# Two transformer blocks on one core: late norm sums, value projections in rows of tokens, and another order of the mixer's jobs

## The chip, the core and the metric

The kernel runs on one core of a Trainium2 chip. The metric is the device time of one execution in microseconds (us). The core has TensorE (PE, matrix products), VectorE (DVE), ScalarE (ACT), GpSimd (POOL) and SyncE (SP, which here only issues DMAs). Each engine works through its own queue in order and waits on semaphores for the others; transfers from HBM run on 16 DMA engines.

## The reference

256 tokens of width 2048 go through two blocks in float32. The first has what the change touches; the second (a convolution and RWKV-7 mixer and a gated feed-forward part) stays as it is.

```python
h = rmsnorm(x, g_mix) * (1 + sc1) + sh1            # sc1, sh1 from silu(c) @ w_ada + b_ada
proj = h @ w_in
q_a, k_a, v_a, q_b, k_b, v_b, qi, ki, wi, g_a, g_b = jnp.split(proj, offsets, axis=-1)
y_a = stick_breaking_attention(q_a, k_a, v_a)       # 8 heads of 128
y_b = dsa_attention(rope(q_b), rope(k_b), v_b,      # 8 heads of 128, the 64 best keys
                    rope(qi), rope(ki), wi)         # by an index score of 16 heads of 64
merged = sigmoid(g_a) * (y_a @ w_a) + sigmoid(g_b) * (y_b @ w_b)
x = x + (1 + gt1) * (merged @ w_o)
```

A stick-breaking head needs `z = q k^T`, the softplus of z under a mask, running sums of it over the keys (products with a triangle), an exponential, and the product with v. A sparse head needs `q k^T` plus the mask of the 64 best keys, a softmax, and the product with v.

## The kernel before, in words

Activations lie with features on the 128 partitions and the 256 tokens on the free axis. Each weight matrix comes in blocks of 2048 x 128, loaded by one DMA of 1 MB (`raw`) and split into a high and a low part (`whi` on ScalarE, `wlo` on VectorE). A **job** is one such block: for each of 16 slices of the contraction three matmuls (high x high, high x low, low x high), 48 in all, into one PSUM bank; then its epilogue `epi` is called. Four slices make a **unit** (12 matmuls). `run` writes out the program: unit by unit it first splits weights some units ahead (`pump_hi`, `pump_lo`), then emits the matmuls, at a job's end its epilogue, and then calls `advance`, one **tick**.

Side work is written as Python generators in the list `fill`. `advance` takes the first three of the list and lets each do one step, if its time has come; `yield n` means "not before n ticks from now", a bare `yield` one tick. So the order of instructions on every engine is fixed when the program is written; a step's instructions stand on TensorE's queue between two units. A job's `pre` is called before its first matmul; `drain(gens)` in it calls `advance` until the named generators have ended, with no unit between those ticks. The background generator `bg` (other modulation vectors, on VectorE) makes a step in four ticks of seven.

The **prologue** (`start`) computes the modulation columns sc1 and sh1 from 33.5 MB of `w_ada` in four groups of eight steps (`kq`) of two 0.5 MB chunks `ch` each, held in eight buffers. A step is done either by TensorE (those in `PEQ`; `m<-cb,ch`) or by VectorE (`fa<-ch,csil,fa`; its sums are closed on TensorE, `m<-cm,fa`, after the last such step). `finish(g)` makes four of the 16 slices of h. The generator `side` runs beside it, two steps for each `kq`: the sums of squares of x for the norm (squares on ScalarE, additions on GpSimd, sums over features on TensorE, inverse root on VectorE, `rx`), then `rope_tables` (cosines and sines, in 33 steps). The first jobs of w_in are in the group `h1`, whose units are interleaved with the last three groups: they pull the prologue along by `need`.

Jobs then follow in the order key/weight job, eight index query jobs, eight stick-breaking heads (q, k, v job each), eight sparse heads (q, k, v), gates with `w_a` and `w_b`, `w_o`. `v_epi` copies the values, turns them with two TensorE transposes a tick later, and copies them again. `sb_gen(h)` and `dsa_gen(h)` are created when a head's v job ends and wait until its values are there.

Of the kernel before, what the change touches and what calls it, by code (L numbers as in the profile page):

```python
# [123 lines left out]


class Job:
    def __init__(self, chunks, mv, n, epi, pre=None, outs=None, group=None, need=None, gate=False):
        self.chunks = chunks
        self.mv = mv
        self.n = n  # L130
        self.epi = epi
        self.pre = pre
        self.nk = sum(c[1] for c in chunks)
        self.outs = outs or [(0, self.nk)]
        self.group = group
        self.need = need
        self.gate = gate


class Builder:  # L140
# [258 lines left out]
    def run(self, jobs):  # L399
# [121 lines left out]
        for i, (j, ci, o, k, n) in enumerate(order):  # L521
            if j.gate:
                if (i - gi) % 4 == 0:
                    gated(i)
                continue
            if j.group == "h1":
                j.need(k + n)
                pump_dma()
            if self.lazy:
                pump_hi(i + LEAD)  # L530
                pump_lo(i + LOMIN)
                for x in range(LOMIN + 1, LEAD):
# [12 lines left out]
            hi, lo = wt.pop(i)  # L545
            for q in range(n):
                kk = k + q
                oi = next(x for x, (a0, n0) in enumerate(j.outs) if a0 <= kk < a0 + n0)
                a0, n0 = j.outs[oi]
                out = ps[id(j)][oi][:, :j.n]  # L550
                mh, ml = j.mv(kk)
                self.mm(out, hi[:, q], mh, start=(kk == a0), stop=False)
                self.mm(out, hi[:, q], ml, start=False, stop=False)
                self.mm(out, lo[:, q], mh, start=False, stop=(kk == a0 + n0 - 1))
            if k + n == j.nk:
                j.epi(*ps.pop(id(j)))
            self.advance()
# [167 lines left out]
    def kw_epi(self, ps):  # L725
        ki = self.rope(ps, self.cosi, self.sini)
        self.kz = [self.a(), self.a()]
        self.nc.vector.memset(self.kz[1][:, :S], 0.0)
        self.ts(self.kz[0][:, :S], ki[:, :S], self.pcol("kmask"))
        self.act(self.kz[1][32:64, :S], ki[0:32, :S])  # L730
        self.act(self.kz[1][96:128, :S], ki[64:96, :S])
        w = self.a()
        self.act(w[32:48, :S], ps[32:48, :S])

        def g():
            yield
            p = self.mps()
            for t in range(2):
                self.nc.tensor.transpose(p[:, 16 * t:16 * t + 16], w[32:48, 128 * t:128 * t + 128], self.ident[32:48, 32:48])
            self.wi = self.cp.tile([128, 32], F32, name="wi")  # L740
            self.ts(self.wi, p[:, 0:32], 0.25)
            yield

        self.g_kw = self.later(g())
# [43 lines left out]
        self.busy = False  # L788
        yield

    def v_epi(self, store, h):
        def epi(ps):
            t = self.a()
            self.act(t[:, :S], ps[:, :S])

            def g():
                yield
                p = self.mps()
                for k in range(2):
                    self.nc.tensor.transpose(p[:, 128 * k:128 * k + 128], t[:, 128 * k:128 * k + 128], self.ident)  # L800
                o = self.a()
                self.act(o[:, :S], p[:, :S])
                store[h] = o
                yield
            self.later(g())
        return epi

    def sb_gen(self, h):
# [26 lines left out]
        self.mm(cp[:, 256:384], tri, sp[:, 256:384])  # L835
        self.sub(zs, zs, cp[:, :384])
        self.act(zs, zs, AF.Exp)
        yield 3
        self.pv(zs, v, self.ya, h)
        yield  # L840

# [7 lines left out]

    def dsa_gen(self, h):  # L850
        scale = 128.0 ** -0.5
        while h not in self.vb or self.g_idx in self.fill:
            yield
        q, k, v = self.qb.pop(h), self.kb.pop(h), self.vb.pop(h)
        lp = self.mps()
# [24 lines left out]
    def build_mixer(self):  # L880
# [13 lines left out]
        self.qi, self.qa, self.ka, self.va, self.qb, self.kb, self.vb = {}, {}, {}, {}, {}, {}, {}  # L894
        self.ya, self.yb = {}, {}

        wj(self.kw_epi, group="h1")
        for j in range(8):
            wj(self.qi_epi(j), group="h1" if j < 3 else None)

        def start_idx():
            self.drain([self.g_kw])
            self.g_idx = self.later(self.index_gen())
# [15 lines left out]
        def with_gen(epi, make, lst):  # L919
            def f(ps):  # L920
                epi(ps)
                lst.append(self.later(make()))
            return f

        for hh in range(NH):
            wj(cp_epi(self.qa, hh), pre=start_idx if hh == 0 else None)
            wj(cp_epi(self.ka, hh))
            wj(with_gen(self.v_epi(self.va, hh), lambda hh=hh: self.sb_gen(hh), sbg))
        for hh in range(NH):
            wj(rp_epi(self.qb, hh))  # L930
            wj(rp_epi(self.kb, hh))
            wj(with_gen(self.v_epi(self.vb, hh), lambda hh=hh: self.dsa_gen(hh), dsg))

        mg = {}
        self.mg = mg
# [838 lines left out]
    def start(self):  # L1774
# [37 lines left out]
        h = self.h  # L1812

        def xnorm():
            pa, pb = self.mps(), self.mps()
            for i in range(KT):
                q = self.a()
                self.act(q[:, :S], x[i][:, :S], AF.Square)
                if i % 4:
                    nc.gpsimd.tensor_add(t[:, :S], t[:, :S], q[:, :S])  # L1820
                else:
                    t = q
                if i % 4 == 4 - 1:
                    for p, o in ((pa, 0), (pb, 128)):
                        self.mm(p[:, 0:64], t[:, o:o + 128], self.ones[:, 0:64], start=i == 4 - 1, stop=i == KT - 1)
                    yield
            v, y, q = self.tiny(), self.tiny(), self.tiny()
            self.ts(v[:, 0:1], pa[:, 0:1], 1.0 / D, EPS)
            self.ts(v[:, 1:2], pb[:, 0:1], 1.0 / D, EPS)
            self.rsq(y[:, :2], v[:, :2], q[:, :2], 3)  # L1830
            rps = self.bcast(y)
            self.rx = self.a()
            self.act(self.rx[:, :S], rps[:, :S])
            yield

        accs, sums = {}, {}
        side = self.chain(xnorm(), self.rope_tables())

        def accumulate(g, kq):
            if kq == 0:  # L1840
# [14 lines left out]
            for mi, m in enumerate((1, 0)):  # L1855
                for j in range(4):
                    o = ps[:, 256 * mi + 64 * j:256 * mi + 64 * j + 64]
                    c = slice(128 * j, 128 * j + 128)
                    if kq in pe:
                        b = 128 * PEK.index(kq)  # L1860
                        for kk in range(2):
                            self.mm(o, chunks[g, kq, m][:, kk, c], cb[:, b + 64 * kk:b + 64 * kk + 64],
                                    start=kq == pe[0] and kk + mi + j == 0, stop=kq == 7 and kk + mi + j == 5)
                    if kq == dve[-1]:
                        self.mm(o, accs[g][m][:, c], self.ones[:, 0:64], start=False, stop=kq == 7 and mi + j == 4)
            for _ in range(SPE if kq in pe else 0):
                next(side, None)
            fetch()
# [19 lines left out]
        def steps():  # L1888
# [8 lines left out]
                yield  # L1897
            for _ in side:
                pass
            nc.sync.dma_start(self.cm[:, 256:NCM], self.ap["cmask"][:, 256:NCM])  # L1900
            self.x = None
            self.enter(1)
# [48 lines left out]


_W = {
    "w_in": (89, 128, KT, 128), "w_ada": (D, 6 * D), "w_a": (KT, 128, 8, 128), "w_b": (KT, 128, 8, 128),
    "w_o": (KT, 128, KT, 128), "w_up": (2 * FT, 128, KT, 128), "w_down": (NQ, KT, 128, FQ, 128),
    "w_in_2": (52, 128, KT, 128), "lora": (8, 128, 4, 128), "w_out_2": (KT, 128, KT, 128),
    "w_gu_2": (2 * FT, 128, KT, 128), "w_down_2": (NQ, KT, 128, FQ, 128),
# [24 lines left out]
def layout(inp):  # L1982
# [11 lines left out]
    wi = w[:, o[8]:o[9]]  # L1994
    kw = np.concatenate([ki[:, :32], wi, np.repeat(z, 16, 1), ki[:, 32:], np.repeat(z, 32, 1)], 1)
    qi = w[:, o[6]:o[7]].reshape(D, 8, 2, 2, 32).transpose(0, 1, 3, 2, 4).reshape(D, 1024)
    cols = [kw, qi]
    for h in range(NH):
        for s in range(3):
            cols.append(w[:, o[s] + 128 * h:o[s] + 128 * h + 128])  # L2000
    for h in range(NH):
        for s in range(3, 6):
            cols.append(w[:, o[s] + 128 * h:o[s] + 128 * h + 128])
    for s in (9, 10):
        for j in range(KT):
            cols.append(w[:, o[s] + 128 * j:o[s] + 128 * j + 128])
    out["w_in"] = _blocks(np.concatenate(cols, 1))
    out["w_ada"] = np.ascontiguousarray(g["w_ada"][0])
    out["w_a"] = _blocks(g["w_a"][0])
    out["w_b"] = _blocks(g["w_b"][0])  # L2010
# [82 lines left out]
```

## Time and profile before

| what | us |
|---|---|
| median of 3 runs | 3025.03 |
| the runs | 3024.79, 3025.03, 3029.89 |
| profiled execution, its own time | 3029.85 |
| span from first to last instruction | 3028.1 |

The rows further down come from that one profiled execution. A row of a timeline has the start, the time, engine, source line, operation, output<-inputs, shapes and count, and in brackets how long the engine was idle before it and what ended that. Nearly all matmuls have line 271, a helper; `m` are small PSUM tiles, `g` those of jobs. A float32 matmul stands as two instructions. A matmul's busy time overlaps the next one's, so the rate is read from starts or from the pieces of the chain.

### The profile page before, as it was taken

The page shows a single profiled execution, that of the slowest core. Times are in us where ns is not written, and L with a number is a line of the kernel's source. Part 1 is how long each engine was busy: PE and PEld are TensorE (multiplying, and loading weights), DVE is VectorE, ACT ScalarE, POOL GpSimd, SP SyncE. Part 2 cuts the span into 40 slices and gives each one's busy share as a digit, 9 for nine tenths or more (in the row PEclk, how much of TensorE's full clock was granted, in tenths as well). Part 3 has the DMA queues.
Part 4 walks back from the last instruction along what each step waited for, and adds up shares of the span by engine and source line. Part 5 has one row for each costly group of instructions (what it writes and reads, how often), then busy time and mean ns, then how long its engine had stood idle before and what let it go on. Part 6 is the DMA issues. An engine that isn't in the chain of part 4 may idle for free.

```text
span 3028.1 us, 66212 instructions
## 1 busy us (share of the span) xinstructions
PE 2975.4 (98%) x27088; PEld 2944.3 (97%) x27088; DVE 2185.2 (72%) x4516; ACT 1573.9 (52%) x3214; POOL 161.6 (5%) x295
## 2 busy tenths in 40 slices
PE   7999999999999999999999999999999999999997
PEld 7999999999999999999999999999999999999997
DVE  6787798677887667676677867777577556566565
ACT  1256544444556556565567545444565555454454
POOL 1000000000210000000002000001000000000002
PEclk9799999999999999999999999999999999999998
DMA  9867677787875554555545433233445454554543
GB/s 343 307 219 250 220 261 264 255 288 263 316 261 184 179 190 168 202 181 177 189 163 188 160 116 116 89 108 125 140 151 197 167 198 173 202 181 167 198 162 129
DMA packets 123473, 594.18 MB, mean 196 GB/s; under 512 B 12832, under 2 KB 19360, under 8 KB 81056
## 3 DMA queue, kind: packets, MB, share of 16 engines
q1 hardware_dynamic: 103200, 518.60, 48.9%
q0 software_dynamic: 19968, 71.35, 7.4%
q8 instruction: 212, 3.47, 0.4%
q14 instruction: 93, 0.76, 0.1%
HBM read 585.68 MB, written 4.21 MB: 195 GB/s over the span
## 4 chain that ended last, share of the span: by engine, by line
PE 95%; DVE 3%; DMA 2%; ACT 0%; issue 0%; SPq 0%; POOL 0%; DVEq 0%; ACTq 0%; POOLq 0%
PE g L271 85%; PE m L271 9%; DMA ch<-w_ada 1%; DVE wlo L242 0%; DMA a<-xT 0%; DVE a L262 0%; DVE a L242 0%; PE m L1414 0%; DVE o L242 0%; DMA cm<-cmask 0%; DVE fa L262 0%; DMA raw<-w_up 0%; ACT a L229 0%; DVE acc L262 0%; DVE p L242 0%
## 5 line engine op out<-in xcount | busy, mean ns | idle before, releaser
L271 PE MATMUL g<-a,whi 128*128 128x256 f32 (+2 forms) x11920 | 2187.2, 285 | 2.4 <-ACT a L229 1.9
L271 PEld LDWEIGHTS g<-a,whi 128*128 128x128 f32 x11920 | 1845.7, 189 | 14.1 <-ACT a L229 2.0
L271 PE MATMUL g<-a,wlo 128*128 128x256 f32 (+3 forms) x5960 | 1684.1, 283 | 1.5 <-DVE wlo L242 1.5
L229 ACT ACTIVATE whi<-raw 128x512 fp32r<-128x512 f32 (+1 forms) x1852 | 1093.4, 617 | 519.3 <-PE g L271 495.5
L242 DVE TENSOR_TENSOR wlo<-raw,whi 128x512 fp32r<-128x512 f32 (+1 forms) x1852 | 1212.9, 681 | 132.2 <-ACT whi L229 130.8
L271 PEld LDWEIGHTS g<-a,wlo 128*128 128x128 f32 x5960 | 1127.1, 189 | 2.9 <-DVE wlo L242 2.6
L271 PE MATMUL g<-h,whi 128*128 128x256 f32 x1408 | 248.9, 281 | 0.0
L271 PE MATMUL g<-ex,whi 128*128 128x258 f32 x1232 | 227.1, 284 | 0.0
L271 PEld LDWEIGHTS g<-h,whi 128*128 128x128 f32 x1408 | 214.9, 188 | 0.0
L271 PE MATMUL g<-h,wlo 128*128 128x256 f32 x704 | 197.8, 281 | 0.0
L271 PEld LDWEIGHTS g<-ex,whi 128*128 128x128 f32 x1232 | 191.3, 190 | 0.0
L262 DVE SCALAR_TENSOR_TENSOR acc<-ra,csil,acc 128x512 f32<-128x512 f32 x240 | 182.1, 759 | 3.9 <-DMA ra<-w_ada 3.9
L229 ACT ACTIVATE a<-a 128x256 f32<-128x256 f32 (+5 forms) x303 | 120.9, 410 | 106.4 <-DVE a L242 79.6
L271 PE MATMUL g<-ex,wlo 128*128 128x258 f32 x616 | 174.9, 284 | 0.3 <-DVE wlo L242 0.3
L262 DVE SCALAR_TENSOR_TENSOR a<-a,pc 128x255 f32<-128x255 f32 (+5 forms) x340 | 163.6, 482 | 5.5 <-ACT a L229 0.5
L229 ACT ACTIVATE a<-a,pc 128x256 f32<-128x256 f32 (+2 forms) x214 | 116.8, 547 | 58.6 <-DVE a L242 53.2
L242 DVE TENSOR_TENSOR a<-g,rb 128x258 f32<-128x258 f32 x80 | 34.1, 426 | 154.4 <-PE g L271 154.4
L635 POOL TENSOR_TENSOR a<-a 128x256 f32<-128x256 f32 x59 | 54.1, 927 | 1673.1 <-ACT a L229 1618.2
L229 ACT ACTIVATE a<-g 128x256 f32<-128x256 f32 (+3 forms) x121 | 46.2, 384 | 179.8 <-PE g L271 179.6
L271 PEld LDWEIGHTS g<-h,wlo 128*128 128x128 f32 x704 | 135.2, 192 | 0.0
L271 PE MATMUL m<-p 64*64 64x64 f32 x3328 | 133.6, 219 | 0.1
L262 DVE SCALAR_TENSOR_TENSOR a<-a 128x256 f32<-128x256 f32 (+3 forms) x275 | 116.6, 424 | 11.7 <-ACT a L229 7.7
(171 smaller groups left out, 1848.3 us busy)
## 6 DMA issues: line engine op xcount, KB each, us to landing
raw<-w_in SPq DMA_DIRECT2D x141, 1024.0 KB, 5.8
raw<-w_up SPq DMA_DIRECT2D x88, 1024.0 KB, 4.9
raw<-w_down SPq DMA_DIRECT2D x128, 704.0 KB, 4.1
raw<-w_gu SPq DMA_DIRECT2D x88, 1024.0 KB, 4.9
ra<-w_ada POOLq DMA_DIRECT2D x128, 512.0 KB, 5.4
ch<-w_ada SPq DMA_DIRECT2D x64, 512.0 KB, 7.5
raw<-w_o SPq DMA_DIRECT2D x16, 1024.0 KB, 7.2
raw<-w_out SPq DMA_DIRECT2D x32, 512.0 KB, 3.6
```

What stands on the lines that cost most here:

```text
L229: self.nc.scalar.activation(out, in_, f, **kw)
L242: self.nc.vector.tensor_tensor(out, a, b, op)
L262: self.nc.vector.scalar_tensor_tensor(out, a, s, b, op0, op1)
L271: self.nc.tensor.matmul(out, l, r, start=start, stop=stop)
L635: self.nc.gpsimd.tensor_tensor(q[:, :n], q[:, :n], acc[:, :n], ALU.add)
```

## The change

1. `xnorm` no longer sums over features as squares come in: it keeps four partial sums and issues the eight matmuls once seven steps of the prologue have been emitted.
2. `rope_tables` isn't part of `side` any more. It is put into `fill` when the prologue's last step has been emitted, and the key/weight job drains it first.
3. Values: four heads make one **wide** job. The stationary operand is h (128 tokens), the moving one a slice of 512 weight columns; two PSUM banks take 128 tokens each. Six matmuls a slice, a unit is one slice, 16 units a job. Its epilogue copies eight pieces of 128 x 128; the transposes are gone.
4. Order: q and k of heads 0 and 1 (these four jobs are now the group `h1`), values of heads 0 to 3, key/weight job, eight index query jobs, q and k of heads 2 and 3, values of 4 to 7, q and k of 4 to 7; then values of sparse heads 0 to 3, their q and k, values of 4 to 7, their q and k. The index generator starts with head 2's q job.
5. `sb_gen(h)` and `dsa_gen(h)` are created in the epilogue of the head's k job; `dsa_gen` waits for the key instead of the value.
6. Two waits in ticks: four instead of one before the weight transposes of the key/weight job, four instead of three before the last product of a stick-breaking head.

```diff
+            if j.wide:
+                kk, last = k // 4, k + n == j.nk
+                wh, wl = (t.rearrange("p q c -> p (q c)") for t in (hi, lo))
+                mh, ml = j.mv(kk)
+                for t in range(2):
+                    out, c = ps[id(j)][t], slice(128 * t, 128 * t + 128)
+                    self.mm(out, mh[:, c], wh, start=kk == 0, stop=False)
+                    self.mm(out, mh[:, c], wl, start=False, stop=False)
+                    self.mm(out, ml[:, c], wh, start=False, stop=last)
...
         def g():
-            yield
+            yield 4
             p = self.mps()
...
+    def v_epi(self, store, h0):
+        def epi(*ps):
+            for h in range(4):
+                o = store[h0 + h] = self.a()
+                for t in range(2):
+                    self.act(o[:, 128 * t:128 * t + 128], ps[t][:, 128 * h:128 * h + 128])
...
         self.act(zs, zs, AF.Exp)
-        yield 3
+        yield 4
         self.pv(zs, v, self.ya, h)
...
-        while h not in self.vb or self.g_idx in self.fill:
+        while h not in self.kb or self.g_idx in self.fill:
...
+        def vj(s, h0, pre=None):
+            w = ap["w_v"][2 * s + h0 // 4]
+            jobs.append(Job([(w[g], KT) for g in range(4)], mvh, S, self.v_epi(self.vb if s else self.va, h0), pre,
+                            outs=[(0, 2 * KT), (2 * KT, 2 * KT)], wide=True))
+
+        def sbq(hh, group=None, pre=None):
+            wj(cp_epi(self.qa, hh), pre=pre, group=group)
+            wj(with_gen(cp_epi(self.ka, hh), lambda hh=hh: self.sb_gen(hh), sbg), group=group)
+
+        sbq(0, "h1")
+        sbq(1, "h1")
+        vj(0, 0)
+        wj(self.kw_epi, pre=lambda: self.drain([self.g_rope]))
+        for j in range(8):
+            wj(self.qi_epi(j))
+        sbq(2, pre=start_idx)
+        sbq(3)
+        vj(0, 4)
+        for hh in range(4, NH):
+            sbq(hh)
         for hh in range(NH):
-            wj(cp_epi(self.qa, hh), pre=start_idx if hh == 0 else None)
-            wj(cp_epi(self.ka, hh))
-            wj(with_gen(self.v_epi(self.va, hh), lambda hh=hh: self.sb_gen(hh), sbg))
-        for hh in range(NH):
+            if hh % 4 == 0:
+                vj(1, hh)
             wj(rp_epi(self.qb, hh))
-            wj(rp_epi(self.kb, hh))
-            wj(with_gen(self.v_epi(self.vb, hh), lambda hh=hh: self.dsa_gen(hh), dsg))
+            wj(with_gen(rp_epi(self.kb, hh), lambda hh=hh: self.dsa_gen(hh), dsg))
...
         def xnorm():
-            pa, pb = self.mps(), self.mps()
+            sums = []
             for i in range(KT):
                 q = self.a()
                 self.act(q[:, :S], x[i][:, :S], AF.Square)
                 if i % 4:
+                    t = sums[-1]
                     nc.gpsimd.tensor_add(t[:, :S], t[:, :S], q[:, :S])
                 else:
-                    t = q
+                    sums.append(q)
                 if i % 4 == 4 - 1:
-                    for p, o in ((pa, 0), (pb, 128)):
-                        self.mm(p[:, 0:64], t[:, o:o + 128], self.ones[:, 0:64], start=i == 4 - 1, stop=i == KT - 1)
-                    yield
+                    yield
+            while len(seen) < 7:
+                yield
+            pa, pb = self.mps(), self.mps()
+            for i, t in enumerate(sums):
+                for p, o in ((pa, 0), (pb, 128)):
+                    self.mm(p[:, 0:64], t[:, o:o + 128], self.ones[:, 0:64], start=i == 0, stop=i == 4 - 1)
+            yield
             v, y, q = self.tiny(), self.tiny(), self.tiny()
...
-        side = self.chain(xnorm(), self.rope_tables())
+        seen = []
+        side = xnorm()
...
+            self.g_rope = self.later(self.rope_tables())
```

The weights of w_in are laid out anew to match (73 blocks and `w_v` of 4 x 4 blocks of 1 MB).

## Rows read from the trace of the kernel before

**Rows 1.** Page, part 1: busy time (share of the span) x instructions.

```profile
PE 2975.4 (98%) x27088; PEld 2944.3 (97%) x27088; DVE 2185.2 (72%) x4516; ACT 1573.9 (52%) x3214; POOL 161.6 (5%) x295
```

**Rows 2.** Timeline of TensorE in the prologue.

```profile
48.37 20.71 PE L271 MATMUL m<-cb,ch 128*128 128x64 f32 x96 [0.90 <-DMA ch<-w_ada]
...
74.96 7.74 PE L271 MATMUL m<-cb,ch 128*128 128x64 f32 x64
...
95.12 7.06 PE L271 MATMUL m<-cb,ch 128*128 128x64 f32 x32 [3.27 <-DMA ch<-w_ada]
...
102.51 0.41 PE L271 MATMUL g<-a,wlo 128*128 128x256 f32 x1
...
104.43 0.41 PE L271 MATMUL g<-a,wlo 128*128 128x256 f32 x1
104.64 13.75 PE L271 MATMUL m<-cb,ch 128*128 128x64 f32 x64
```

**Rows 3.** Windows: length, then busy time of each engine, granted clock, DMA share, GB/s.

```profile
14.00:76.00 62.00, 56.84 (x262) 56.12 (x262) 46.38 (x107) 11.05 (x24) 7.08 (x10) 1.00 0.99 357
76.00:89.60 13.60, 13.03 (x112) 12.58 (x111) 12.69 (x22) 3.73 (x8) 0.00 (x0) 1.00 1.05 387
89.60:120.30 30.70, 27.15 (x126) 27.00 (x127) 20.47 (x36) 2.44 (x5) 1.60 (x3) 0.50 0.92 334
138.00:172.00 34.00, 33.22 (x281) 33.20 (x282) 33.35 (x67) 15.91 (x27) 3.17 (x6) 1.00 0.67 233
350.00:504.00 154.00, 154.00 (x1301) 153.59 (x1300) 133.37 (x268) 74.80 (x163) 13.19 (x25) 1.00 0.72 243
2236.60:2246.90 10.30, 6.53 (x27) 6.08 (x27) 9.65 (x28) 5.23 (x13) 0.00 (x0) 0.50 0.00 1
```

**Rows 4.** All waits of TensorE, 138 to 771 us: total, times, longest.

```profile
PE m L739 <- ACT a L229: 2.0, 1, 2.0
PE m L271 <- ACT sc L229: 1.5, 1, 1.5
```

**Rows 5.** Chain that ended last, in a sparse head: start, time, what.

```profile
372.10 7.08 PE g L271 x60
379.18 0.22 PE m L800 x2
```

**Rows 6.** Timeline of VectorE in the prologue.

```profile
22.33 0.16 DVE L258 TENSOR_SCALAR ty<-m 128x1 f32<-128x1 f32 x1 [10.02 <-PE m L271]
...
38.78 1.54 DVE L262 SCALAR_TENSOR_TENSOR fa<-ch,csil,fa 128x512 f32<-128x512 f32 x2 [0.98 <-DMA ch<-w_ada]
```

**Rows 7.** The chain that ended last, in the second block's mixer.

```profile
1636.60 9.03 PE g L271 x72
```

**Rows 8.** Groups by line and shape, TensorE, 1637 to 1645 us: busy, mean ns.

```profile
L271 PE MATMUL g<-a,whi 128*128 128x272 f32 x23 | 4.5, 288 | 0.0
```

**Rows 9.** Timeline of ScalarE: the copy at a stick-breaking head's q job's end.

```profile
238.67 0.38 ACT L229 ACTIVATE a<-g 128x256 f32<-128x256 f32 x1 [1.41 <-PE g L271]
```

**Rows 10.** The chain that ended last, around the first stick-breaking head.

```profile
202.46 0.49 ACT sc L229
...
202.97 1.28 ACT L229
...
206.09 0.53 ACT sc L229
...
206.65 0.57 DVE sc L262
...
207.25 0.90 DVE sc L242 x4
```

**Rows 11.** Timeline of TensorE at the second feed-forward part's start.

```profile
2241.72 0.58 PE L271 MATMUL g<-a,whi 128*128 128x258 f32 x1 [1.95 <-ACT a L229]
```

**Rows 12.** Timeline of VectorE: a sparse head's rotation.

```profile
371.47 1.29 DVE L242 TENSOR_TENSOR a<-g,a 64x256 f32<-64x256 f32 x3 [1.08 <-PE g L271]
372.80 0.42 DVE L242 TENSOR_TENSOR a<-a 128x256 f32<-128x256 f32 x1
```

More of the change, by code (lines that the diff above doesn't have):

```diff
@@ L126, with __init__ @@
 class Job:
-    def __init__(self, chunks, mv, n, epi, pre=None, outs=None, group=None, need=None, gate=False):
+    def __init__(self, chunks, mv, n, epi, pre=None, outs=None, group=None, need=None, gate=False, wide=False):
         self.chunks = chunks
@@ L137, in __init__ @@
         self.gate = gate
+        self.wide = wide
 class Builder:
@@ L545, in run @@
             hi, lo = wt.pop(i)
-            for q in range(n):
+            if j.wide:
[7 more added lines that the diff above has]
+                    self.mm(out, ml[:, c], wh, start=False, stop=last)
+            for q in range(0 if j.wide else n):
                 kk = k + q
@@ L789, in index_gen @@
         yield
[L791 to L796, printed above, removed]
-                yield
[L798 to L805, printed above, removed]
+    def v_epi(self, store, h0):
[4 more added lines that the diff above has]
+                    self.act(o[:, 128 * t:128 * t + 128], ps[t][:, 128 * h:128 * h + 128])
         return epi
@@ L895, in build_mixer @@
         self.ya, self.yb = {}, {}
-        wj(self.kw_epi, group="h1")
-        for j in range(8):
-            wj(self.qi_epi(j), group="h1" if j < 3 else None)
         def start_idx():
@@ L1865, in accumulate @@
                         self.mm(o, accs[g][m][:, c], self.ones[:, 0:64], start=False, stop=kq == 7 and mi + j == 4)
+            seen.append((g, kq))
             for _ in range(SPE if kq in pe else 0):
@@ L1953 @@
 _W = {
-    "w_in": (89, 128, KT, 128), "w_ada": (D, 6 * D), "w_a": (KT, 128, 8, 128), "w_b": (KT, 128, 8, 128),
+    "w_in": (73, 128, KT, 128), "w_v": (4, 4, 128, KT, 128), "w_ada": (D, 6 * D), "w_a": (KT, 128, 8, 128), "w_b": (KT, 128, 8, 128),
     "w_o": (KT, 128, KT, 128), "w_up": (2 * FT, 128, KT, 128), "w_down": (NQ, KT, 128, FQ, 128),
@@ L1996, in layout, with sb @@
     qi = w[:, o[6]:o[7]].reshape(D, 8, 2, 2, 32).transpose(0, 1, 3, 2, 4).reshape(D, 1024)
-    cols = [kw, qi]
+    cols = []
+    def sb(h, parts):
+        for s in parts:
+            cols.append(w[:, o[s] + 128 * h:o[s] + 128 * h + 128])
+    for h in range(2):
+        sb(h, (0, 1))
+    cols += [kw, qi]
+    for h in range(2, NH):
+        sb(h, range(2))
     for h in range(NH):
[L1999 to L2002, printed above, removed]
+        for s in range(3, 5):
             cols.append(w[:, o[s] + 128 * h:o[s] + 128 * h + 128])
@@ L2007, in layout @@
     out["w_in"] = _blocks(np.concatenate(cols, 1))
+    vs = np.stack([w[:, o[s] + 512 * i:o[s] + 512 * i + 512] for s in (2, 5) for i in range(2)], 0)
+    out["w_v"] = np.ascontiguousarray(vs.reshape(4, 4, 4, 128, 512).transpose(0, 1, 3, 2, 4)).reshape(4, 4, 128, KT, 128)
     out["w_ada"] = np.ascontiguousarray(g["w_ada"][0])
```

## The prediction

> **What bounds the kernel now.** I read the profile's page first, and in it the line of the engines: TensorE is busy for 98% of the span [rows 1], so a microsecond that TensorE waits or is spared is a microsecond of the total, and what other engines save counts only where TensorE waits for them. TensorE's lines of the timeline show what that busy time is made of. In the prologue (to about 137 us) it multiplies the modulation weights, which arrive by DMA. Work on 64 columns took 20.71 us for 96 instructions at 48 us, 13.75 for 64 at 104 us, and 7.74 for 64 at 75 us [rows 2]: 0.215, 0.215 and 0.121 us each. The windows name the cause for the later stretch: granted clock 0.50, the 1.2 GHz level, from 89.6 to 120.3 us; for 14 to 76 us their column says 1.00, but the spacing is that of the lower level, and I believe the spacing [rows 2, 3]. Transfers run at 357 to 387 GB/s, and TensorE's waits at 48.37 and 95.12 us are for the weights [rows 2, 3]. So transfers and a TensorE at its lower level share the bound there, and VectorE (12.69 of 13.6 us busy before 89.6) is close behind. After 138 us the list of waits holds two entries for TensorE up to 771 us, 2.0 and 1.5 us [rows 4]: the mixer is one dense stream, 60 matmuls in 7.08 us, 0.118 us each [rows 5].
>
> **Late norm sums.** Before, TensorE's sums come first, and VectorE waits 10.02 us for them, until 22.33 [rows 6]. That wait cost little: TensorE goes from the sums straight into the first group's 96 instructions of 0.215 us, whose weights by the order of the requests and the transfer rate land at 20.7 us at the earliest (an estimate). Now the sums (8 matmuls, 16 instructions, 3.4 us at the lower level) stand behind the seventh step of the first group. TensorE can start the 96 up to 1.8 us earlier, at 20.7 to 22.5 us; 96 x 0.215 = 20.6 brings it to 41.3 to 43.1, the sums to 44.7 to 46.5. Behind them on VectorE's queue stand the small square-root chain (13 instructions like that of 0.16 us, 2.1 to 2.5 us) and then the eighth step's four accumulations (two took 1.54 us [rows 6]: 3.0 us), which formerly were done before; half of the group's closing matmuls (8 x 0.215 = 1.7) come after that. The first group closes at 52 to 53.7 instead of 47.47 (48.37 less the wait of 0.90 [rows 2]): 4.5 to 6.2 us later. The buffers of the eighth step are freed as late, so transfers pause too, and later waits (3.27 us at 95.12) don't give it back. I take +5. Bounds: up to +11, if the later end falls wholly on the lower clock level; down to -9, the floor of the transfers below. VectorE's table work, gone from here, was beside these waits and is worth nothing where the weights or TensorE end last.
>
> **The two waits that go.** The key/weight job now has three more ticks before its small transposes (-2.0), and the first stick-breaking head one more before its last product (-1.5) [rows 4].
>
> **Values in rows of tokens.** The 32 transposes disappear: two took 0.22 us [rows 5], so -3.5 us. ScalarE makes as many copies, of half the width, as before. The bytes are the same (16 loads of 1 MB on SP's queue before and after; POOL's queue has its 12 additions at the same place). 768 matmuls of 256 columns become 384 of 512. At the lower clock nine of 256 columns took 1.92 us (102.51 to 104.43), 0.213 each, at the full one 0.118 [rows 2, 5]: the part that scales with the clock is 0.095, the fixed part at most 0.023. A matmul of 512 columns thus takes 0.213 to 0.236 us: a gain of 0 to 8.9 us over 384. A stretch of 260 and 272 columns took 9.03 us for 72, 0.125 each, wider and longer by about the same share [rows 7, 8], which is near the end without gain; I take -3.
> The row for a stream of 256 columns is 0.118 us [rows 5]. The Trainium skill's page "TensorE: Matmul & The Clock Gate" (Back-to-back issue gap) gives a sustained 131 ns per matmul at N=512. By the row's extrapolation the term is -3; by the page it would be 384 x (0.236 - 0.131) = -40 us, an estimate from that page; no run here shows 512 columns.
>
> **Rotary tables after the prologue.** They are 33 steps of VectorE with four sines on ScalarE, one step a tick, a tick after each unit of 12 matmuls (or 6 wide ones). From their start 12 units of the first four jobs and 16 of the first value job remain: 28 steps, under about 39 us of TensorE's work, whose cover is VectorE's share left from splitting weights; it was 98% busy at 138 to 172 us [rows 3] with the query jobs' rotations, which now come later. So the steps are free as far as they fit. They don't fit: the key/weight job must drain the rest first, six ticks without a weight matmul between them. In that same drain the first two stick-breaking heads, waiting for values since the last unit, do their first, second (+2 ticks) and third stage (+6 ticks). The third stage's matmuls are queued on TensorE ahead of the key/weight job's, and wait for VectorE, which waits for ScalarE. **This is the first new wait.** Its length, from the value job's last matmul: eight value copies, 2.0 (each between half and all of 0.38 [rows 9]); scaled copy and absolute value for two heads, 4 x 0.45 = 1.8; table load, exp, table load, log (1.28 + 0.5 + 1.28 + 0.53 = 3.6) for one head and again for the other, 7.2; VectorE's 0.57 and three of its four mask operations (0.9 for four), 1.25 [rows 10]. Together 12.25, less TensorE's own 16 instructions of 0.11 in it (1.8): 10.5 us. Bounds: 5, if it is no longer than one head's chain at 202.46 to 208.15 less that work; 14 with weight copies and a sine between. TensorE idles so long that its clock should fall: after such a pause the granted clock was 0.50 until 2246.9 with dense work from 2241.72 [rows 3, 11]; 5.2 us at 0.213 instead of 0.118 lose 2.3. I take +2.5 (0 to 4).
>
> **Heads right behind their key jobs.** Before, a head started with the value job, when its key had been ready for four units. Now values come first, the head is created in the epilogue of its key job, and its first products are queued on TensorE in the same tick, right behind that job's last matmul. What they wait for: for stick-breaking heads 2 to 7 ScalarE's copy, 0.38 [rows 9]; plus the tail of the last matmul (0.16, a matmul's 0.28 or 0.29 [rows 8] against a spacing of 0.118) and a handover, 0.6: 6 x 0.6 = +3.5 (2 to 8, behind another ScalarE instruction). For the eight sparse heads VectorE's rotation: it began at 371.47 as soon as TensorE was done (VectorE had waited 1.08 for it) and ended at 373.22, 1.75 us [rows 12]; with the tail and handover 1.95: 8 x 1.95 = +15.6 (12; or 21, if a weight split of 0.7 stands before each). The next job's weight matmuls stand behind these products on TensorE; nothing else can fill the hole. VectorE gets denser in these heads, 8 units each instead of 12, but it was at 133.4 of 154 us [rows 3], and the new holes give it room: 0.
>
> **Sum.** +5 - 2.0 - 1.5 - 3.5 - 3 + 10.5 + 2.5 + 3.5 + 15.6 = +27.1 us on the profiled run's 3029.85 (span 3028.1): 3057. That run lies 4.8 above the median; of the runs shown two are at 3025 and one at 3029.89, two levels that the clock's changes in the prologue could make. I take half of the distance off: 3054.5.
>
> **The rivals.** (a) *The transfers set the prologue's end.* From 14 to 120.3 us they moved 62 x 357 + 13.6 x 387 + 30.7 x 334 GB/s, 37.7 MB, which at 387 takes 97.3 us [rows 3]. Were VectorE's lighter load enough to keep them at that, and TensorE at 2.4 GHz, the prologue would end 9 us earlier, not 5 later: 3054.5 - 14 = 3040.5. For it: VectorE's 93% before 89.6. Against: TensorE's 1.2 GHz spacing as long as it works on 64 columns.
> (b) *The new waits are hidden*: the key is ready when its product comes, and the drain is short. Then +10.5, +2.5, +3.5 and +15.6 fall away: 3022.4, no change that can be told. For it: no wait for a head stands in the list now but one [rows 4]. Against: the order in which instructions are queued, and the 2.0 us that TensorE already waited for a copy one tick old.
> (c) *Wide matmuls are cheap*, the side of faster: if a matmul's time were set by loading its stationary operand and not by its columns, the second 256 would be nearly free. For it: 64 columns took 0.121 us and 256 took 0.118 [rows 2, 5]. Against: 0.125 at 260 and 272 [rows 7]. At 0.118 for 512 columns the gain is 384 x 0.118 = 45 in place of 3: 3012. It turns the sign where a wide matmul takes less than 0.236 - (27.1 + 2.4 + 3)/384 = 0.151 us.
> The Trainium skill's 131 ns, from the section named above, speaks for (c) and would make it 3017, an estimate by that page; the rows at 260 and 272 columns don't agree with it.
>
> **How the numbers follow.** A few tenths of a per cent, say 0.2% or 6 us, is what a measurement of this kernel can tell from none. My forecast has 0.74, (a) 0.10, (b) 0.10, (c) 0.06. The range 3038 to 3066 holds the forecast with the bounds of its larger terms not all at one end, and (a); it leaves out (b), (c) and a little above, 0.2. Slower: the forecast and (a), 0.84; same: most of (b), 0.07; faster: (c) and the rest of (b), 0.09.
>
> **What would show it.** In the list of waits after 138 us: TensorE waiting for VectorE's rotation eight times by some 1.8 us, for ScalarE's copies six times by under 1 us, and one pause of about 10 us in two pieces, for VectorE's masks, before the key/weight job, with a granted clock of 0.50 behind it. The transposes of values and the entries of 2.0 and 1.5 us gone. Matmuls of 512 columns at 0.22 to 0.24 us. In the prologue, the sums after 41 us, and VectorE waiting for them. I am wrong if TensorE's list stays as short as it is now, if the prologue ends well before 120 us, or if the wide matmuls come out under 0.15 us.

## The result, and the profile after

The changed kernel takes 3054.57 us (median of four runs, 3053.14 to 3060.77) against 3025.56 (3024.79 to 3029.89) for the kernel before, run beside it: a ratio of 1.0097, interval 1.0085 to 1.0109. The profiled execution took 3055.18 us, span 3053.3. So it is slower by 29 us, where 3054.5 was forecast. Of all the runs listed in this document, two executions were slow (4105 us of e1, at a granted clock of 0.66, and 3579 us of the kernel before beside e8 to e10, at 0.75): the medians count them, the ratios leave them out. The traces show that the total agrees partly because two terms that nobody forecast cancel; this is the main thing to read below.

The page's first part, to be held against [rows 1]:

```profile
PE 2972.5 (97%) x26672; PEld 2921.9 (96%) x26672; DVE 2187.0 (72%) x4516; ACT 1578.1 (52%) x3215; POOL 159.7 (5%) x295
```

TensorE is still the bound, but it is idle for 81 us of the span, against 53 before. The list of TensorE's waits from 120 to 905 us (line numbers have moved by up to 33) answers to [rows 4]:

```profile
PE m L272 <- DVE a L243: 15.9, 8, 2.2
PE m L272 <- issue: 7.1, 1, 7.1
PE m L272 <- ACT a L230: 3.5, 4, 1.6
PE m L272 <- DVE fa L263: 1.7, 1, 1.7
PE m L272 <- DVE sc L243: 1.7, 1, 1.7
```

The two entries of before are gone. In their place stand eight waits for VectorE's rotation (15.9 us in all), the pause before the key and weight job in two pieces (7.1 and 1.7), and 3.5 us for ScalarE's copies of keys (heads 4 to 7, 0.5, 0.5, 1.6 and 0.9 us). The wait for `fa` belongs to the prologue. How one of the eight comes about is seen on VectorE's timeline, and behind it on TensorE's:

```profile
419.74 0.42 DVE L243 TENSOR_TENSOR a<-m,a 128x256 fp32r<-128x256 f32 x1
420.08 0.68 DVE L243 TENSOR_TENSOR wlo<-raw,whi 128x512 fp32r<-128x512 f32 x1
420.79 1.30 DVE L243 TENSOR_TENSOR a<-g,a 64x256 f32<-64x256 f32 x3
422.12 0.43 DVE L243 TENSOR_TENSOR a<-a 128x256 f32<-128x256 f32 x1
```
```profile
422.69 1.54 PE L272 MATMUL m<-a 128*128 128x128 f32 x4 [2.00 <-DVE a L243]
```

The four instructions from 420.79 to 422.56 are the rotation of the key; TensorE's products with that key are next in its queue and start at 422.69. The pause before the key and weight job is in the chain that ended last:

```profile
164.58 1.12 ACT a L230 x6
...
168.10 1.28 ACT L230
...
169.94 1.28 ACT L230
...
171.77 1.28 ACT L230
...
173.61 1.28 ACT L230
...
175.46 0.57 DVE sc L263
...
176.49 2.05 PE m L272 x8
```

Copies of values, then exp and log for two heads in turn with a table load of 1.28 us ahead of each, then VectorE's masks: the chain that the prediction laid out. The windows answer to [rows 3] (columns as there):

```profile
88.30:112.20 23.90, 23.90 (x114) 23.90 (x114) 19.55 (x35) 2.45 (x5) 0.00 (x0) 0.50 1.02 374
172.00:180.00 8.00, 5.56 (x24) 5.32 (x25) 5.71 (x17) 6.34 (x7) 0.53 (x1) 0.50 0.12 50
350.00:504.00 154.00, 142.06 (x954) 131.74 (x953) 115.68 (x230) 67.64 (x144) 11.13 (x21) 0.96 0.65 221
```
```profile
390.00:396.00 6.00, 5.19 (x29) 5.17 (x30) 4.82 (x13) 1.62 (x5) 0.00 (x0) 0.72 0.69 255
420.00:427.00 7.00, 5.00 (x27) 4.65 (x27) 5.15 (x12) 2.69 (x8) 0.00 (x0) 0.76 0.58 213
```

The second fence is the surprise: around a wait of 2 us the granted clock falls, for 3.4 us each time, to 0.50 (6 us at a mean of 0.72 are 2.6 at full and 3.4 at half). There are six such stretches between 392 and 532 us, behind six of the eight waits, and in the kernel before none [rows 3]. In such a stretch TensorE does half of what it would: up to 1.7 us each, some 10 us in all (an estimate from these rows).

In the prologue, TensorE's timeline answers to [rows 2]:

```profile
22.42 20.72 PE L272 MATMUL m<-cb,ch 128*128 128x64 f32 x96 [22.42 <-DMA ch<-w_ada]
42.93 3.62 PE L272 MATMUL m<-cm,a 128*128 128x64 f32 x16
48.97 1.22 PE L272 MATMUL m<-cm,ty 128*128 128x128 f32 x4 [2.42 <-DVE ty L263]
50.42 3.67 PE L272 MATMUL m<-cm,fa 128*128 128x64 f32 x16 [0.23 <-DVE fa L263]
...
123.59 1.10 PE L272 MATMUL m<-cm,fa 128*128 128x64 f32 x8 [1.74 <-DVE fa L263]
```

The sums stand at 42.93, the wait for the square-root chain behind them, and the first group closes at 54 us, as written down. And the 512-column multiplications:

```profile
151.90 0.40 PE L272 MATMUL g<-wlo,a 128*128 128x512 f32 x1
152.14 0.63 PE L272 MATMUL g<-whi,a 128*128 128x512 f32 x2
152.60 0.39 PE L272 MATMUL g<-wlo,a 128*128 128x512 f32 x1
```

Three start in the 0.70 us from 151.90: 0.233 us each, nearly twice the 0.118 of 256 columns [rows 5]. The Trainium skill's 131 ns at N=512 ("TensorE: Matmul & The Clock Gate", Back-to-back issue gap) doesn't agree with these rows.

Where the time went, by three rows of one view (first and last start of a group): the prologue's closing matmuls (`fa`), the first feed-forward part's first (`ex`), and those with the `h` tiles of the last down projection. First a fresh profile of the kernel before (span 3030.0), then the changed kernel:

```profile
L271 PE MATMUL m<-cm,fa x64: 222/421/422, 45.3 to 123.5; 128*128 128x64 f32 x64
L271 PE MATMUL g<-ex,whi x1232: 276/282/367, 864.1 to 1563.2; 128*128 128x258 f32 x176
L271 PE MATMUL g<-h,whi x1408: 281/281/282, 2392.0 to 3009.2; 128*128 128x256 f32 x176
```
```profile
L272 PE MATMUL m<-cm,fa x64: 219/421/473, 50.4 to 124.4; 128*128 128x64 f32 x64
L272 PE MATMUL g<-ex,whi x1232: 276/282/366, 900.5 to 1593.6; 128*128 128x258 f32 x176
L272 PE MATMUL g<-h,whi x1408: 276/276/287, 2422.5 to 3032.7; 128*128 128x256 f32 x176
```

From the last `fa` to the first `ex`, called the mixer's length from here on, it is 740.6 us before and 776.1 after: +35.5. From `ex` to the end of the span it is 2165.9 before and 2152.8 after: -13.1, although TensorE has the same instructions there in the same order. The `h` matmuls take 276 ns in place of 281. Measured from start to start they lie 113.4 and 117.8 ns apart, in every one of their four stretches; over 2112 of them that is 9.3 of the 13.1 us. Where the other 3.8 us lie stays open.

### The profile page after: what moved, and what is told of

Read it like the earlier page. It is cut to its first block, busy times and chain, and to the rows that moved or that the text cites. A ratio compares the mean times of both kernels' runs of the same rounds, so it can differ in the third digit from the quotient of the medians.

```text
span 3053.3 us, 65407 instructions
## 1 busy us (share of the span) xinstructions
PE 2972.5 (97%) x26672; PEld 2921.9 (96%) x26672; DVE 2187.0 (72%) x4516; ACT 1578.1 (52%) x3215; POOL 159.7 (5%) x295
## 4 chain that ended last, share of the span: by engine, by line
PE 94%; DVE 3%; DMA 1%; ACT 1%; issue 0%; SPq 0%; DVEq 0%
PE g L272 84%; PE m L272 9%; DMA ch<-w_ada 1%; DVE a L243 1%; DVE wlo L243 1%; PE m L1428 0%; DVE o L243 0%; ACT sc L230 0%; ACT L230 0%; DMA cm<-cmask 0%; ACT a L230 0%; DVE acc L263 0%; DVE a L263 0%; DVE p L243 0%; DVE sc L243 0%
## 5 line engine op out<-in xcount | busy, mean ns | idle before, releaser
L272 PE MATMUL g<-a,whi 128*128 128x256 f32 (+3 forms) x11408 | 2102.2, 286 | 2.1 <-ACT a L230 1.9
L272 PEld LDWEIGHTS g<-a,whi 128*128 128x128 f32 x11408 | 1774.2, 190 | 14.1 <-ACT a L230 2.0
L272 PE MATMUL g<-a,wlo 128*128 128x256 f32 (+3 forms) x5704 | 1615.4, 283 | 0.9 <-DVE wlo L243 0.9
L272 PEld LDWEIGHTS g<-a,wlo 128*128 128x128 f32 x5704 | 1083.6, 190 | 1.9 <-DVE wlo L243 1.4
L272 PE MATMUL g<-h,whi 128*128 128x256 f32 x1408 | 239.6, 276 | 0.0
L230 ACT ACTIVATE a<-a,pc 128x256 f32<-128x256 f32 (+2 forms) x214 | 117.2, 549 | 63.7 <-DVE a L243 53.7
L230 ACT ACTIVATE a<-g 128x256 f32<-128x256 f32 (+4 forms) x137 | 46.5, 364 | 165.4 <-PE g L272 165.0
```

The costliest lines, as they stand in the source:

```text
L230: self.nc.scalar.activation(out, in_, f, **kw)
L272: self.nc.tensor.matmul(out, l, r, start=start, stop=stop)
```

## The experiments

All runs, each against the kernel before on the same chip (mixer length and `h` duration from the run's profile). The kernel before had medians of 3026.80 us beside e1 to e3, 3026.97 beside e4 to e7 and 3025.24 beside e8 to e10:

| run | median us | ratio to before, interval | mixer us | h, ns |
|---|---|---|---|---|
| e0_before_again | 3031.72, one run | | 740.6 | 281 |
| e1_dsa_wait | 3028.88 | 1.0006 [0.9997, 1.0016] | | |
| e11_dsa_look | 3031.03, one run | | 750.6 | 276 |
| e2_no_drain | 3055.22 | 1.0093 [1.0077, 1.0108] | 773.4 | 276 |
| e3_early_sums | 3043.75 | 1.0056 [1.0041, 1.0071] | 775.8 | 276 |
| e4_spaced | 3024.28 | 0.9992 [0.9983, 1.0001] | 743.6 | 276 |
| e5_best | 3025.99 | 0.9998 [0.9989, 1.0008] | 743.4 | 281 |
| e6_values_only | 3027.01 | 1.0000 [0.9990, 1.0009] | 740.3 | 281 |
| e7_slot | 3015.79 | 0.9965 [0.9956, 0.9975] | 740.7 | 276 |
| e8_after_held | 3054.63 | 1.0097 [1.0080, 1.0114] | 775.4 | 276 |
| e9_values_held | 3014.39 | 0.9966 [0.9955, 0.9978] | 739.2 | 276 |
| e10_best_held | 3026.77 | 1.0004 [0.9994, 1.0013] | 741.7 | 281 |

**e0_before_again**: the kernel before, unchanged.

> The kernel before, unchanged, for a second profile. In the changed kernel 12 of the 37 us lost by the end of the mixer came back in the two feed-forward parts, whose instructions are the same; the matmuls of the second down projection ran at 0.113 instead of 0.118 us. Theory A (a spread between executions): this profile shows a rate between or like the changed kernel's. Theory B (where buffers lie in SBUF or how the queues stand to each other, which is fixed by the program): 0.118 us again, within 0.001.

Its rows are shown above. The `h` matmuls are at 281 ns again, so as far as two profiles can tell, that rate belongs to the program and not to the run.

**e1_dsa_wait and e11_dsa_look**: the same kernel twice; the trace is e11's.

```diff
         while h not in self.kb or self.g_idx in self.fill:
             yield
+        yield 2
```

> The changed kernel, but a sparse head waits two ticks after its key before its first product. Theory A (the product stood on TensorE behind the key job and waited for VectorE's rotation, and the holes also pulled the clock down): the eight waits of 15.9 us vanish and the six stretches of 3.4 us at 1.2 GHz (20.5 us, worth 20.5 x 0.45 = 9 us) with them, so about 25 us less than the changed kernel, 3030 us. Theory B (the stretches at 1.2 GHz come from something else, as the denser work on VectorE): only the 16 us come back, 3039 us. Theory C (the holes only gave VectorE room that it needs): TensorE waits for split weights instead, less than 8 us come back, above 3046 us.

> The kernel after with two ticks for the rotation of the sparse heads' keys, looked at once more for its trace, since the first profile of it was of a disturbed run. Theory A (the 26 us are 15.9 us of waits and the six stretches of half clock behind them): no entry for VectorE's rotation in TensorE's waits, no granted clock of 0.50 between 380 and 540 us, and 24 to 27 us less from the end of the prologue to the first feed-forward part. Theory B (part of the 26 us is the feed-forward parts' rate or the prologue): the waits gone, but less than 20 us of it there.

Two ticks gave back 25.7 us of 29 (27 when each kernel is held against the one before on its own chip). In the trace (first group of `ex`, waits, and the window of the sparse heads):

```profile
L272 PE MATMUL g<-ex,whi x1232: 276/282/367, 878.3 to 1572.5; 128*128 128x258 f32 x176
```
```profile
PE m L272 <- issue: 7.1, 1, 7.1
PE m L272 <- ACT a L230: 3.4, 4, 1.6
...
PE m L272 <- DVE a L243: 0.3, 1, 0.3
```
```profile
350.00:504.00 154.00, 152.97 (x1098) 143.21 (x1097) 131.14 (x264) 76.02 (x164) 12.68 (x24) 1.00 0.73 248
```

The entry of 15.9 us is down to 0.3, the clock is 1.00 throughout, and the mixer is 25.5 us shorter (the last `fa` starts at 127.7 here). The waits account for 15.6 of it; the other 10 is what the six half-clock stretches were estimated at, and they went with the waits. Theory A stands. The pause before the key and weight job is untouched.

**e2_no_drain**: the first two heads wait until the tables are done.

```diff
-        while h not in self.va:
+        while h not in self.va or self.g_rope in self.fill:
             yield
```

> The changed kernel, but stick-breaking heads also wait until the rotary tables have ended, so that no stage of theirs falls into the drain. Theory A (the drain's pause is the wait of the first two heads' masks): the waits of 7.1 and 1.7 us go, and with them the stretch at 1.2 GHz after them, 10 to 11 us less than the changed kernel, 3044 us. Theory B (the tables themselves are too much for VectorE at this place): TensorE waits there for split weights or for the tables, less than 4 us come back, above 3050 us.

The time did not move, which is theory B's forecast, but not for the reason that it gave. Windows of this run:

```profile
174.00:178.00 4.00, 1.34 (x12) 1.17 (x11) 1.24 (x5) 3.94 (x5) 0.00 (x0) 1.00 0.14 56
178.00:182.00 4.00, 1.42 (x11) 1.25 (x10) 1.79 (x8) 3.37 (x5) 0.00 (x0) 0.66 0.00 0
```

The hole has moved behind the first 48 weight matmuls: ScalarE is busy for 3.94 and 3.37 of 4 us with the two heads' exps, logs and table loads, and weight splits queue behind them. TensorE still waits there, 2.7 and 2.6 us, for the heads' masked values, and 6.8 us at half clock follow. So the pause does not need the drain. The trace suggests two heads' chains on ScalarE side by side, with too little of TensorE's work between their stages; e4 spaces them out.

**e3_early_sums**: the norm sums multiplied at once, as before the change.

```diff
-            sums = []
+            pa, pb = self.mps(), self.mps()
...
                 if i % 4 == 4 - 1:
+                    for p, o in ((pa, 0), (pb, 128)):
+                        self.mm(p[:, 0:64], t[:, o:o + 128], self.ones[:, 0:64], start=i == 4 - 1, stop=i == KT - 1)
                     yield
-            while len(seen) < 7:
-                yield
```

> The changed kernel with the norm sums where they were, ahead of the first weights; the tables stay behind the prologue. Theory A (late sums close the first group later and so cost time): the first group closes near 47.5 instead of 54 us, and 2 to 7 us come back, 3048 to 3053 us. Theory B (late sums are hidden behind the transfers of weights, which set the end): no change, 3054 to 3056 us. Theory C (late sums help, as TensorE starts on the weights sooner): 2 us or more above the changed kernel.

10.8 us came back, more than any of the theories gave the late sums. The mixer is as long as in the changed kernel (775.8); the last `fa` starts at 115.6 instead of 124.4, so 8.8 of it are in the prologue. The granted clock differs there too: 13.7 us at 0.50 in e3, 23.9 in the changed kernel. That the sums cost time at the same clock is seen in e8 below.

**e4_spaced and e5_best**: both new waits given room; e5 with the early sums of e3 too.

```diff
+        while h not in self.va or self.g_rope in self.fill:
             yield
+        yield 1 + 8 * (h == 1)
...
-        yield 4
+        yield 12 if h < 2 else 4
...
         while h not in self.kb or self.g_idx in self.fill:
             yield
+        yield 2
```

> The kernel after, with the rotation of the sparse heads' keys given two ticks, and the first two stick-breaking heads started one and nine ticks after the rotary tables are done, with twelve ticks in place of four for their middle stage, so that the chip's own work stands between their stages. Theory A (the mixer lost its time to these two places and to the clock that fell in them): the sparse heads give back the 26 us of the run that gave them their two ticks alone, the pause before the key and weight job gives back its 8.8 us of waits and about 4 to 5 us of half clock: 3054.6 - 26 - 13 = 3015 to 3019 us, with no granted clock of 0.50 between 130 and 560 us. Theory B (the pause only moves, because the two heads' work on ScalarE has to be done somewhere): 3026 to 3029 us, with waits of the same length later than 180 us.

> As the run with the two waits spaced out, and the four sums of the first norm again multiplied at once. Theory A (the late sums cost their 10.8 us in the prologue whatever follows): 3054.6 - 39 - 11 = 3004 to 3008 us, faster than both kernels. Theory B (the time gained in the prologue is taken up by the waits behind it, the transfers among them): 3012 to 3019 us.

e4 came out 5 us above theory A's range, e5 18 us above. The mixer was 743.6 and 743.4 us, 7 less than with the sparse heads' ticks alone, so the spacing gave back about that much of the pause. The rest moved, as theory B had it: e4 still waits 2.6, 1.1 and 1.9 us between 173 and 183 us, with 3.4 us at 0.50 behind it.

```profile
PE g L272 <- DVE wlo L243: 4.0, 3, 2.6
PE m L749 <- ACT a L230: 1.9, 1, 1.9
```

Of e5's waits the longest are:

```profile
PE g L272 <- DVE wlo L243: 2.9, 1, 2.9
PE m L272 <- ACT a L230: 0.8, 2, 0.4
PE m L749 <- ACT a L230: 0.8, 1, 0.8
```

A weight split comes late, and the granted clock is 0.50 for 10.2 us around it. Early sums moved the last `fa` from 124.7 (e4) to 118.3 (e5), yet e5 is not faster as a whole: its `h` matmuls are at 281 ns, e4's at 276. From the first `ex` to the end e5 takes 2164.1 us and e4 2154.0. So the rate behind the mixer decides as much as these edits; e7 tests what sets it.

**e6_values_only**: early sums, tables in the prologue and the index jobs first, as before the change; of the change the values in rows, with the key and weight job's longer spacing. The heads are still created behind their key jobs, with one tick more (stick-breaking) and two (sparse).

```diff
+        wj(self.kw_epi, group="h1")
+        for j in range(8):
+            wj(self.qi_epi(j), group="h1" if j < 3 else None)
+        for hh in range(NH):
+            if hh % 4 == 0:
+                vj(0, hh, pre=start_idx if hh == 0 else None)
+            sbq(hh)
...
+        side = self.chain(xnorm(), self.rope_tables())
```

> Of the change only the values in rows of tokens (and the key and weight job's longer spacing): the norm sums are early, the tables made in the prologue and the index jobs first, as in the kernel before; the heads get the ticks that the value job gave them. Theory A (what the change gains lies in the values: 3.5 us of transposes, 1.7 us of wide multiplications and the 2.0 us wait, with the prologue of before): 3025.6 - 7 = 3017 to 3020 us if the feed-forward parts run at the rate of before, 3008 to 3011 us if they run at that of after (113 in place of 118 ns for each multiplication with the h tiles). Theory B (the reordering was what let the values pay, or the wide job brings waits of its own): 3024 to 3030 us.

3027.0, in theory B's range. The mixer is 740.3 us, 0.3 less than before. The values save 3.5 us of transposes and 1.2 of wide matmuls, and the old waits of 2.0 and 1.5 are gone; new waits take that back:

```profile
PE m L272 <- ACT a L230: 3.9, 5, 2.3
```

All five stand before a stick-breaking head's first product, which waits for ScalarE's copy of its key and not of its values. The longest, in the chain that ended last:

```profile
223.81 0.61 ACT whi L230
224.43 0.28 ACT a L230
...
224.75 0.92 PE m L272 x4
```

Adding a late weight split of 0.9, rotations of 0.6 and one half-clock stretch of 3.4 us, little is left. So in this order, with heads behind their key jobs, the values in rows gain next to nothing in all. What they are worth with heads created as before stays open.

**e7_slot**: the kernel before, with one activation buffer held from the prologue until the first feed-forward part.

```diff
+        self.held = self.a()
+        nc.vector.memset(self.held[:, 0:1], 0.0)
...
+                self.nc.vector.memset(self.held[:, 0:1], 0.0)
```

> The kernel before with nothing of the change: one more activation buffer is held from the prologue to the first feed-forward part, so that later activation tiles lie in other buffers; TensorE has exactly the same multiplications in the same order, VectorE two settings of 128 elements more. Theory P (where the activation tiles lie decides at which of two rates the feed-forward parts run): the h multiplications change from 117.8 to 113.4 ns or the parts around them shift, and the time moves by some us, down to about 3014 us. Theory Q (TensorE's own run of instructions decides it): they stay at 117.8 ns and the time at 3025 to 3027 us.

It is 11 us faster than the kernel before (3015.79 against 3026.97; 8 to 13 by the interval):

```profile
L271 PE MATMUL g<-h,whi x1408: 276/276/288, 2385.9 to 2993.8; 128*128 128x256 f32 x176
```

Theory P's forecast holds. TensorE's instructions are the same; VectorE has the two short settings more. Against e0's profile 8.4 us lie behind the first `ex` (2157.5 against 2165.9). The last `fa` is 7.1 us earlier too (116.4 against 123.5), with a shorter stretch at 0.50 in the prologue, so the two profiles differ by more than the rate.

**e8_after_held, e9_values_held, e10_best_held**: the same held buffer in the changed kernel, in e6 and in e5.

> The kernel after with one more activation buffer held from the prologue to the first feed-forward part, as in the run that did this to the kernel before; nothing else. Theory P (where activation tiles lie picks one of two rates for the h multiplications, and the 12 us that the kernel after got back behind the mixer are that and no effect of its mixer): the rate is drawn anew; 3053 to 3056 us if it stays 113.4 ns, 3062 to 3066 us if it falls to 117.8 ns; the delay at the end of the mixer, 37 us to the kernel before, stays in both within 5 us. Theory Q (the reordered mixer itself leaves TensorE's queue at the faster rate): 113.4 ns and 3053 to 3056 us.

> The run with the values in rows alone, with one more activation buffer held in the same way. Theory P: 117.8 or 113.4 ns, drawn anew, and 3027 or 3016 to 3018 us with it; a mixer as long as without it within 2 us. Theory Q (the values' job leaves the rate of before): 117.8 ns and 3025 to 3029 us.

> The run with early sums and the spaced waits, with one more activation buffer held in the same way. Theory P: 117.8 or 113.4 ns, drawn anew, and 3026 or 3015 to 3017 us with it; the mixer stays 2 to 3 us longer than that of the kernel before, since the values in rows bring it nothing. Theory Q (the rate goes with the order of the mixer's jobs): no clear forecast, as this order has shown both rates; 3026 us.

e8 stayed at 276 ns and e10 at 281. e9 changed from 281 to 276, and its median by -12.6 us (e6, then e9):

```profile
L272 PE MATMUL g<-h,whi x1408: 281/281/287, 2384.8 to 3003.5; 128*128 128x256 f32 x176
```
```profile
L272 PE MATMUL g<-h,whi x1408: 276/276/283, 2387.7 to 2995.7; 128*128 128x256 f32 x176
```

From the first start to the last it is 618.7 us in e6 and 608.0 in e9. TensorE's instructions are the same in both, and in the built programs the `h` and weight tiles that these matmuls read and the PSUM banks that they write lie at the same addresses, as they do in the kernels before and after. Only activation tiles lie elsewhere, and VectorE has the two settings. That so small an edit can switch the rate is shown by e7 and e9; that it does so by the tiles' places, and not by what else shifts with it, is argued. Theory Q's alternative, that the mixer's order or TensorE's own instructions set it, falls: e5 and e4 have nearly one order and different rates, e6 and e9 the same instructions. Which places give which rate is not settled.

e7 and e9 beat both kernels, by a third of a per cent, and neither by the change's own means.

## Why the prediction was right, and where only by balance

**Late norm sums: the mechanism holds, the size hangs on the clock.** Predicted +5 (bound +11). The order of events is as written, and the first group closes at 54 us (52 to 53.7 was forecast; the lower end of that sum adds up to 51.5). Against the same kernel with early sums it costs 8.8 us of prologue and 10.8 of the whole (e3). Against the two profiles of the kernel before the prologue ends only 0.9 to 2.2 us later, for another reason: there the clock stayed at 0.50 for 30.7 us [rows 3], and in e3, e5, e6, e7 and e10, with the same early sums, for a stretch of 13.7. In e9 it was 30.7 us again, and the last `fa` at 122.5. Early sums end at 116 to 118 us or at 122 to 124, with the clock; late ones ended at 124 to 128 in every profile. e8, with late sums, had the short stretch too and still ended as late (its `fa` and a window, then e3's `fa`):

```profile
L272 PE MATMUL m<-cm,fa x64: 220/372/476, 52.0 to 124.3; 128*128 128x64 f32 x64
100.60:114.20 13.60, 10.67 (x50) 10.71 (x51) 11.59 (x23) 2.44 (x5) 0.00 (x0) 0.50 1.02 367
```
```profile
L272 PE MATMUL m<-cm,fa x64: 274/421/423, 43.3 to 115.6; 128*128 128x64 f32 x64
```

So where both have the short stretch, late sums cost 6 to 9 us. What makes the clock fall early or late there was not tried.

**The two waits that go, and the transposes.** All three (-2.0, -1.5, -3.5) are gone from the trace as sized, and no wait for a copy of values stands in the changed kernel's list beyond the pause. That e6 gains nothing from the same three does not speak against them: there heads behind their key jobs brought waits of their own.

**Wide matmuls.** -3 was taken; 384 x (0.236 - 0.233) = -1.2 by the three starts shown, inside its bounds. Rival (c) would have needed 0.151 us.

**The pause before the key and weight job.** Predicted 10.5 in two pieces; measured 7.1 and 1.7, so 8.8. The clock behind it: predicted 2.5; the window at 172 to 180 us has 5.56 us of TensorE's work at 0.50, half of which, 2.8, is loss (an estimate). e2 adds that the pause does not need the drain.

**Heads behind their key jobs.** Predicted 3.5 and measured 3.5 for the copies, but in four entries of 0.5 to 1.6 us rather than six of 0.6, so the equal sum is chance; predicted 15.6 and measured 15.9 for the eight rotations. The step missing from the sum is what these holes do to the clock: some 10 us more, as e11 shows. The prediction charged the clock for the long pause only.

**Nothing behind the mixer.** The sum had no term there, and the changed kernel got 13.1 us back, 9.3 of them in the `h` matmuls. e7 and e9 show that a gain of this kind needs no change of the mixer at all. That the changed kernel's own gain came by its tile places is argued from them and not shown; e8, which moved its tiles, stayed at the faster rate.

**The balance.** Predicted for the mixer +22.1, measured +35.5; predicted behind it 0, measured -13.1; the prologue +5 against +0.9. Their sum, 23.3 us on a fresh profile's span of 3030.0, is what the spans show, and it was 25.2 on the profile that the prediction used. On that profile the prediction's sum is +27.1; the 2.4 us that it then took off, a guess at the two levels of the kernel before, cover the 1.9 between them. The signs and the waits were right. The total was right to a microsecond because two errors of 13 us met and the smaller ones fell well: that is luck.

Of the rivals, (a) fails: the prologue did not end 9 us earlier but later, and the weights did not set its end, since e3 ends it 8.8 us earlier with the same weights. (b) fails by the list of waits: none of the four was hidden. (c) fails by the 0.233 us.

## What to carry to other kernels

Where a consumer is queued right behind the producer of its operand, count the engines' handover for every such pair and then the clock: here eight holes cost 15.9 us of waiting and some 10 of half speed, and two ticks of spacing took nearly all of both away. A reordering is to be judged by stages: compare the length of each stage, also of those that didn't change, before a total is read as the effect of an edit. And before a third of a per cent is credited to an edit, shift the buffers of the old kernel once; here that alone moved the median by 11 us.

## What the hardware showed unexpectedly

Identical multiplications with identical operands ran at 281 or at 276 ns (117.8 or 113.4 ns apart), the same over all four stretches of 528 in each profile and in both profiles of the kernel before; holding one more, unrelated activation buffer switched it (e7, e9) or not (e8, e10).

Holes of about 2 us in dense work brought stretches of 3.4 us at a granted clock of 0.50, the 1.2 GHz level: six for eight holes in the changed kernel's sparse heads, none once the holes were closed (e11). And with early sums the prologue has two clock patterns, about 14 or 31 us at 0.50, worth some 6 us of its end; the spread of repeated runs of the kernel before (3022.6 to 3032.4 us) would fit them, which no run here isolates.
